# Attention query, key and gate projections of a hybrid encoder block: from 24 full blocks to twelve units of seven half-size products

## The chip, the cores and the metric

The kernel runs on one core of a Trainium2 chip. The metric is the device time of one execution in microseconds (us), taken as the median of several runs. A core has a matrix engine (TensorE, PE in the profile, with its weight loads as PEld), a vector engine (VectorE, DVE), a scalar engine (ScalarE, ACT), GpSimd (POOL) and a sync engine (SyncE, SP). Each takes its own instructions in program order and waits for others by semaphores. SP and POOL issue most of the DMA transfers between device memory (HBM) and the on-chip memory (SBUF); matmul results go to eight banks of PSUM, which PE writes and DVE and ACT read.

## The reference

One layer of an encoder over 512 tokens with 2048 features, in float32. Cut to what matters here:

```python
h = rms_norm(x, norm_mix_w)
q_a, k_a, v_a, q_g, k_g, v_g, r_g, gate_lr = split_cols(h @ w_in, IN_SPLITS)
y_a = chunked_band_attention(q_a, k_a, v_a, att_rel_bias)     # 16 heads of 64
o_g = rms_norm(gated_linear_attention(q_g, k_g, v_g, log_a), gla_norm_w)
y_g = o_g * silu(r_g)                                         # 4 heads, values of 256
x = x + concat([y_a, y_g]) @ w_out
u_gate, u_val = split(causal_depthwise_conv(rms_norm(x, norm_ffn_w) @ w_ffn_up))
x = x + (gelu(u_gate) * u_val) @ w_ffn_down
x = x + sigmoid(rms_norm(x, norm_ple_w) @ w_ple_gate) * (p @ w_ple_proj)
return rms_norm(x, final_norm_w)
```

`q_a`, `k_a`, `v_a` and `r_g` are 1024 features wide each: eight blocks of 128 features for the queries, eight for the keys, eight for the gates `r_g`. With 512 tokens and chunks of 64, the band of nine chunks is causal by chunks: a tile of 128 queries sees the keys up to its own end.

## The kernel before

**How a product is made.** Operands are split into a high part in the fp32r format and a low part, the rest. ACT copies the high part, DVE subtracts to get the low part, and PE adds three products: high by high, high by low, low by high. `wtile` (L108) loads a weight tile of 128x1024 (512 KB) and splits it; `mm3` (L122) issues the three matmuls; `proj` (L127) runs them over the 16 feature blocks of the input, so a projection block of 128 features is 48 matmuls of 128x512 over two weight tiles.

**The front.** The scaled input, split, stays in SBUF as `h1` (16 tiles). The row norm `rb` is multiplied in after the products. In order:

- `vproj` (L218) for the linear attention's values, in two halves of features, tokens on the partitions.
- The linear attention: `gla_proj` (L301) makes query, key and decay of a head; `gla_core` (L349) transposes (`pkt`), forms the inner products (`pat`), the chunk states (`pu`, `S1` to `S3`) and the output (`po`), which is normalised and kept in `onorm`. `gate_block` (L252) 0 and 1 stand ahead of the last head's core.
- `vproj` for the attention's values, into `Va`.
- The attention loop over eight head pairs b, written out by hand so that one pair's softmax runs beside the next pair's projections: `att_q(b)`, `att_transpose` of pair b-1, `att_k(b)`, `att_out` of b-1, `att_probs(b)`. `att_q` and `att_k` (L425, L437) project one block each and split the result by head into `Q`, `Kh`, `Kl` so that score matmuls over 128 rows hold both parts of the queries: `Q` of a head has its high part in its own 64 rows and its low part in the others, `Kh` and `Kl` are in both. `att_probs` (L452) multiplies (`psc`, two matmuls for each of four query tiles, 256, 256, 384 and 512 keys wide), adds the bias `E`, takes the maximum (L467), exponentiates on ACT (L470) and normalises (L472). `att_transpose` (L476) turns the probabilities on PE (`ptr`, ten 128x128 transposes for a head) and ACT copies them to `PT` (L486). `att_out` (L491) multiplies with the values in fp32:

```python
for kt in range(TT):
    for s in range(2):
        c0 = (2 * b + s) * 64
        nc.tensor.matmul(py[s * 64:(s + 1) * 64, kt * P:T], Va[:, kt, c0:c0 + 64], PT[s][:, kt, kt * P:T], ...)
```

- Gate blocks 2 and 3 end the loop. Gate blocks 4 to 7 (`pr` at L62) then alternate with the four blocks of the embedding projection `p @ w_ple_proj` (`pp`, `block_product`, L1090), while `mix_pair` (L1113) forms the operands of the out projection and stores them to HBM.

**The later stages.** The out projection (wo), the up projection, three parts of the down projection and the embedding gate (pg) use a form of Strassen's method with seven products. A `Unit` (L615) makes two blocks of 128 output features: its 256x2048 weight matrix and the 2048x512 input are cut in two by two, and seven products of half size (24 matmuls of 128x256 each) replace the eight. The seven, in order, are P1, P2, P6, P5, P7, P3, P4:

```python
PRODUCTS = {"P1": ("L11", "R11", "A"), "P2": ("L12", "R21", "B"), "P6": ("S2", "N2", "A"), "P5": ("S1", "N1", "C"),
            "P7": ("S3", "T3", "A"), "P3": ("S4", "R22", "C"), "P4": ("L22", "T4", "A")}
```

The first entry is the weight operand: L11, L12, L22 are loaded; S1 = L21 + L22 and S3 = L21 + L11 are loaded with a plain transfer on SP and an accumulating one on POOL's queue; S2 and S4 are sums made on DVE. The second entry is the input operand; `store_pair` (L537) makes its seven forms from two rows of blocks (four differences on DVE) and stores them, and `Stage.load` and `Stage.split` (L592, L598) bring them in and split them. The third is the accumulator bank: P1, P6, P7 and P4 add up in accA, and `collect` (L756) copies or adds the bank's state to a quarter of the result `u` after each of the seven. A product that adds to accA therefore waits for the copy of the one before it.

Products form a list of steps. At each step `prep_high` and `prep_low` split the weights of the step after next, `product` issues the 24 matmuls, `collect` follows, and an `agenda` holds other work to be done at the step: rank 0 (transfers) ahead of the split on ACT, rank 1 between the two halves of the split, higher ranks after the product. On DVE, ACT and PE this program order is kept (`InOrder`, L54; all these instructions carry line L62). Weight pages come from a list `free` of nine (`issue`, L645, loads the next weight when a page comes free); six banks hold accumulators and two are for other work.

Of the kernel before, what the change touches and what calls it, by code (L numbers as in the profile page):

```python
# [14 lines left out]
P = 128  # L15
T = 512
# [13 lines left out]
            "P7": ("S3", "T3", "A"), "P3": ("S4", "R22", "C"), "P4": ("L22", "T4", "A")}  # L30
PLAIN = ("P1", "P2", "P6", "P5", "P7", "P3", "P4")
HALVES = ("P1", "P2", "P6", "P7", "P4", "P5", "P3")
RINGS = {"wr": ("r0", "r1", "r2"), "wh": ("h0", "h1", "h2"), "wl": ("l0", "l1", "l2"), "u": ("u2", "u3", "u0", "u1"),
         "c": ("c1", "c2", "c0"), "x": ("x0", "x1")}
# [5 lines left out]
def encoder_block(ctx: ExitStack, tc: tile.TileContext, A, out):  # L40
# [46 lines left out]

    def page(ring, name, dt=F32, shape=(P, 1024)):
        tags = RINGS[ring]
# [128 lines left out]
    def vproj(src, V, start=False):  # L218
        for c in range(2):
            ps = [psum_mm(f"v{c}_{t}") for t in range(TT)]  # L220
            for kp in range(KD // 2):
                first = start and c == 0
                xs = []
                if first and kp > 0:
                    xs.append(load_input(2 * kp))
                hi, lo = wtile(src[c, kp], f"wv{c}_{kp}", 2 if first and kp < 2 else 1,
                               (lambda: xs.append(load_input(0))) if first and kp == 0 else None)
                if first:
                    xs.append(load_input(2 * kp + 1))
                    sq_acc(xs[0], kp == 0)  # L230
                    sq_acc(xs[1], False)
                    if kp == KD // 2 - 1:
                        first_stats()
                for j in range(2):
                    kt = 2 * kp + j
                    wh = hi[:, j * T:(j + 1) * T]
                    wl = lo[:, j * T:(j + 1) * T]
                    for t in range(TT):
                        sl = slice(t * P, (t + 1) * P)
                        nc.tensor.matmul(ps[t], h1[kt][:, 0, sl], wh, start=kt == 0, stop=False)  # L240
                        nc.tensor.matmul(ps[t], h1[kt][:, 0, sl], wl, start=False, stop=False)  # L241
                        nc.tensor.matmul(ps[t], h1[kt][:, 1, sl], wh, start=False, stop=kt == KD - 1)  # L242
            for t in range(TT):
                nc.scalar.activation(V[:, t, c * T:(c + 1) * T], ps[t], AF.Copy, scale=rtok[:, t:t + 1])
# [5 lines left out]
    onorm = []  # L250

    def gate_block(j):  # L252
        pr = psum_mm("pr")
        proj(pr, [A["w_blk"][24 + j, i] for i in range(2)], h1, f"wr{j}")
        r = tp.tile([P, T], F32, tag="sq", name="r")
        nc.vector.tensor_tensor(r, pr, rb, ALU.mult)
        nc.scalar.activation(r, r, AF.Silu)
        nc.vector.tensor_tensor(onorm[j], onorm[j], r, ALU.mult)

    with ExitStack() as mix:  # L260
        vp = mix.enter_context(tc.tile_pool(name="v", bufs=1, side="right"))

        with ExitStack() as gctx:
            gp = gctx.enter_context(tc.tile_pool(name="gla", bufs=1, side="right"))
            reset = gp.tile([P, T], F32, name="reset")
            nc.gpsimd.memset(reset, 1.0)
            nc.gpsimd.memset(reset.rearrange("p (c j) -> p c j", j=CHUNK)[:, :, 0:1], 0.0)
            causal = gp.tile([P, P], I32, name="causal")
            nc.gpsimd.memset(causal, 1)
            nc.gpsimd.affine_select(causal, causal, pattern=[[1, P]], compare_op=ALU.is_ge, fill=0, base=0, channel_multiplier=-1)  # L270
            attn_t = []
            for i in range(2):
                t = gp.tile([P, T], F32, name=f"attnT{i}")
                nc.gpsimd.memset(t, 0.0)
                attn_t.append(t)

            V = vp.tile([P, TT, 1024], F32, tag="V", name="Vg")
            vproj(A["w_v_g"], V, True)
            up2 = gp.tile([P, T], F32, name="up2")[0:32]
            nc.sync.dma_start(up2, A["gate_up"])  # L280

            gl = page("wr", "wgate_r")
            nc.sync.dma_start(gl[:, :256], A["w_gate"])
            glh = page("wh", "glh", F32R)
            nc.scalar.activation(glh[:, KD * 32:KD * 32 + 96], attn_t[0][:, 0:96], AF.Copy)
            gl3 = gl[:, :256].rearrange("p (k r) -> p k r", r=16)
            g3 = glh[:, :KD * 32].rearrange("p (k r) -> p k r", r=32)
            nc.scalar.activation(g3[:, :, 0:16], gl3, AF.Copy)
            nc.vector.tensor_tensor(g3[:, :, 16:32], gl3, g3[:, :, 0:16].bitcast(F32), ALU.subtract)
            plr = psum_mm("plr")  # L290
            for kt in range(KD):
                w = glh[:, kt * 32:kt * 32 + P]
                nc.tensor.matmul(plr, w, h1[kt][:, 0, :], start=kt == 0, stop=False)
                nc.tensor.matmul(plr, w, h1[kt][:, 1, :], start=False, stop=kt == KD - 1)
            lr = gp.tile([P, T], F32, name="lr")[0:32]
            nc.vector.tensor_tensor(lr, plr[0:32, :], rb[0:32, :], ALU.mult)

            def gt(name, tag, bufs=1, cols=T):
                return gp.tile([P, cols], F32, tag=tag, name=name, bufs=bufs)

            def gla_proj(hd):  # L301
                pz = psum_aux("pz")
                nc.tensor.matmul(pz, up2[:, hd * P:(hd + 1) * P], lr, start=True, stop=True)
                b = bgate[:, hd:hd + 1]
                e = gt("e", "e")
                nc.scalar.activation(e, pz, AF.Abs, bias=b)
                nc.scalar.activation(e, e, AF.Exp, scale=-1.0)
                nc.scalar.activation(e, e, AF.Ln, bias=1.0)
                m = gt("lf", "lf")
                nc.vector.tensor_scalar(m, pz, b, 0.0, ALU.add, ALU.min)  # L310
                nc.vector.tensor_tensor(m, m, e, ALU.subtract)
                cs = gt("cs", "cs")
                nc.vector.tensor_tensor_scan(cs, reset, m, 0.0, ALU.mult, ALU.add)
                cs3 = cs.rearrange("p (c j) -> p c j", j=CHUNK)
                last = cs3[:, :, CHUNK - 1:CHUNK]
                eb = gt("eb", "eb", 2)
                nc.scalar.activation(eb, cs, AF.Exp, scale=1.0 / TAU)
                en = gt("en", "en", 2)
                nc.scalar.activation(en, cs, AF.Exp, scale=-1.0 / TAU)
                dd = gt("dd", "dd", 2)  # L320
                nc.vector.tensor_tensor(dd.rearrange("p (c j) -> p c j", j=CHUNK), cs3,
                                        last.broadcast_to([P, NCH, CHUNK]), ALU.subtract)
                nc.scalar.activation(dd, dd, AF.Exp, scale=-1.0 / TAU)
                dec = gt("dec", "dec", 2, NCH)
                nc.scalar.activation(dec, last, AF.Exp, scale=1.0 / TAU)
                dec2 = gt("dec2", "dec2", 2, 2 * NCH + TT)
                de = dec.rearrange("p (t c) -> p t c", c=2)
                to_end = dec2[:, 0:NCH].rearrange("p (t c) -> p t c", c=2)
                from_start = dec2[:, NCH:2 * NCH].rearrange("p (t c) -> p t c", c=2)
                nc.vector.memset(dec2[:, 0:2 * NCH], 1.0)  # L330
                nc.vector.tensor_copy(to_end[:, :, 0:1], de[:, :, 1:2])
                nc.vector.tensor_copy(from_start[:, :, 1:2], de[:, :, 0:1])
                nc.vector.tensor_tensor(dec2[:, 2 * NCH:].rearrange("p (t c) -> p t c", c=1), de[:, :, 0:1], de[:, :, 1:2],
                                        ALU.mult)

                pk = psum_mm("pk")
                proj(pk, [A["w_blk"][20 + hd, i] for i in range(2)], h1, f"wkg{hd}")
                kf = gt("kf", "kf")
                nc.vector.tensor_tensor(kf, pk, rb, ALU.mult)
                nc.vector.tensor_tensor(en, kf, en, ALU.mult)  # L340
                nc.vector.tensor_tensor(dd, kf, dd, ALU.mult)
                pq = psum_mm("pq")
                proj(pq, [A["w_blk"][16 + hd, i] for i in range(2)], h1, f"wqg{hd}")
# [1004 lines left out]
```

## Time and profile before

| | |
|---|---|
| median of 3 runs | 2341.88 us (2335.12 to 2343.68) |
| the profiled execution, its own time | 2345.5 us |
| its span, first to last instruction | 2343.8 us |
| mean granted clock of PE | 0.993 |
| 0 to 338.05 us (values, linear attention) | 338.05 us, PE busy 336.85 |
| 338.05 to 600.47 us (attention loop with gate blocks 2, 3) | 262.42 us, PE busy 261.54 |
| 600.47 to 668.12 us (gate blocks 4 to 7, embedding projection) | 67.65 us, PE busy 66.55 |
| 668.12 to 2343.80 us (out, up, down projections, embedding gate) | 1675.68 us, PE busy 1637.16 |

Times of a trace are from the first instruction of the profiled execution. "PE busy" counts the time in which at least one matmul record is open; records of pipelined matmuls overlap, so the mean length of one is more than its share of the time. A row of the chain gives the start, the length, the engine, the tile written, the line, and how many instructions the piece holds; fp32 matmuls leave two records each. In the list of groups "out<-in" names what is written and read.

### The profile page before, as it was taken

What the parts mean: (1) busy time and instruction counts of PE and PEld (TensorE: products, weight loads), DVE (VectorE), ACT (ScalarE), POOL (GpSimd) and SP (SyncE); (2) the same over time, 40 slices, a digit from 0 to 9 for tenths busy, and PEclk for the clock granted to TensorE, in tenths of its full rate; (3) what the DMA queues carried; (4) which work ended last, traced back from release to release, by engine and by line L of the source; (5) the groups of instructions that cost most, each with busy time, mean ns of one, the idle gap of its engine ahead of it and who ended that gap; (6) DMA issues with size and microseconds to landing.
All of it is one profiled execution on the core that took longest, in us unless ns stands there. A gap on an engine that the chain in (4) does not pass through costs nothing.

```text
span 2343.8 us, 42271 instructions
## 1 busy us (share of the span) xinstructions
PE 2302.1 (98%) x16924; PEld 2162.6 (92%) x16924; DVE 1787.1 (76%) x2459; ACT 1231.7 (53%) x1807; POOL 122.7 (5%) x156
## 2 busy tenths in 40 slices
PE   9999999999999999999999999999999999999996
PEld 8878887777789999999999999999989999999995
DVE  6356326665578898898888888888888787898987
ACT  6344235544465565555555555555564554656655
POOL 0000000000000010000000100000000100001100
PEclk9999999999999999999999999999999999999998
DMA  5222323322788987777777777777875977879994
GB/s 203 83 72 72 101 98 102 92 89 84 235 294 253 299 244 203 211 218 214 214 205 217 207 217 209 209 213 200 252 242 189 311 235 230 280 248 329 280 276 163
DMA packets 172821, 473.99 MB, mean 202 GB/s; under 512 B 18736, under 2 KB 58928, under 8 KB 172624
## 3 DMA queue, kind: packets, MB, share of 16 engines
q1 hardware_dynamic: 148112, 392.64, 48.0%
q0 software_dynamic: 20160, 72.36, 17.9%
q10 hardware_dynamic: 4352, 6.29, 0.8%
q8 instruction: 132, 2.16, 0.4%
q14 instruction: 65, 0.53, 0.1%
HBM read 404.11 MB, written 65.01 MB: 200 GB/s over the span
## 4 chain that ended last, share of the span: by engine, by line
PE 90%; DVE 4%; ACT 3%; DMA 2%; issue 1%; DVEq 0%; SPq 0%; ACTq 0%; POOL 0%; POOLq 0%
PE accA L62 36%; PE accC L62 18%; PE accB L62 9%; PE v L240 2%; PE v L242 2%; PE v L241 2%; PE pr L62 2%; PE pqa L124 1%; PE pqa L123 1%; PE pka L125 1%; PE pqa L125 1%; PE pka L123 1%; PE pka L124 1%; PE pp L62 1%; DMA s<-in_w_dn 1%
## 5 line engine op out<-in xcount | busy, mean ns | idle before, releaser
L62 DVE TENSOR_TENSOR wl<-s,wh 128x1024 fp32r<-128x1024 f32 (+1 forms) x317 | 379.4, 1197 | 62.8 <-ACT wh L62 62.4
L62 DVE TENSOR_TENSOR wl<-l,wh 128x1024 fp32r<-128x1024 f32 (+1 forms) x268 | 319.5, 1192 | 52.1 <-ACT wh L62 51.9
L62 ACT ACTIVATE wh<-l 128x1024 fp32r<-128x1024 f32 (+1 forms) x268 | 276.9, 1035 | 143.5 <-PE accC L62 100.6
L62 ACT ACTIVATE wh<-s 128x1024 fp32r<-128x1024 f32 (+1 forms) x317 | 327.9, 1035 | 28.7 <-DVE s L62 12.0
L62 ACT ACTIVATE u<-accA 128x256 f32<-128x256 f32 x254 | 96.4, 380 | 362.4 <-PE accA L62 362.2
L62 DVE TENSOR_TENSOR s<-s,l 128x1024 f32<-128x1024 f32 (+1 forms) x168 | 200.4, 1193 | 1.4 <-DMA s<-in_w_dn 1.4
L62 PE MATMUL accA<-up_T,wh 128*128 128x256 f32 x1408 | 180.2, 280 | 0.0
L62 PEld LDWEIGHTS accA<-up_T,wh 128*128 128x128 f32 x1408 | 171.9, 188 | 0.0
L62 DVE SCALAR_TENSOR_TENSOR cv<-u,cw,cv 128x511 f32<-128x511 f32 (+1 forms) x176 | 131.6, 748 | 3.1
L663 POOL DMA_DIRECT2D s<-in_w_up x88 | 75.1, 853 | 795.5 <-DMA s<-in_w_up 337.9
L119 DVE TENSOR_TENSOR wv_l<-wv_r,wv_h 128x1024 fp32r<-128x1024 f32 (+1 forms) x34 | 39.5, 1161 | 84.2 <-ACT wv_h L118 84.1
L240 PE MATMUL v<-wv_h,h 128*128 128x512 f32 x256 | 100.5, 393 | 0.0
L242 PE MATMUL v<-wv_h,h 128*128 128x512 f32 x256 | 100.1, 392 | 0.0
L241 PE MATMUL v<-wv_l,h 128*128 128x512 f32 x256 | 99.8, 390 | 0.0
L62 PE MATMUL accA<-up_T,wl 128*128 128x256 f32 x704 | 97.1, 280 | 0.0
L62 PE MATMUL accB<-up_R,wh 128*128 128x256 f32 x704 | 91.7, 282 | 2.0 <-DVE up_R L62 1.3
L62 PE MATMUL accA<-dn_T,wh 128*128 128x256 f32 x704 | 90.7, 281 | 2.7 <-ACT wh L62 2.7
L62 PE MATMUL accA<-up_R,wh 128*128 128x256 f32 x704 | 90.4, 281 | 0.0
L62 PE MATMUL accC<-up_R,wh 128*128 128x256 f32 x704 | 90.0, 280 | 0.0
L62 PE MATMUL accA<-up_N,wh 128*128 128x256 f32 x704 | 90.0, 280 | 0.0
L62 PE MATMUL accC<-up_N,wh 128*128 128x256 f32 x704 | 90.0, 280 | 0.0
L62 PEld LDWEIGHTS accB<-up_R,wh 128*128 128x128 f32 x704 | 87.1, 190 | 2.6 <-DVE up_R L62 1.5
(394 smaller groups left out, 5287.7 us busy)
## 6 DMA issues: line engine op xcount, KB each, us to landing
l<-in_w_up SPq DMA_DIRECT2D x132, 512.0 KB, 5.3
s<-in_w_up SPq DMA_DIRECT2D x88, 512.0 KB, 4.7
s<-in_w_up POOLq DMA_DIRECT2D x88, 512.0 KB, 6.1
l<-in_w_dn SPq DMA_DIRECT2D x56, 448.0 KB, 4.9
l<-in_w_out SPq DMA_DIRECT2D x28, 512.0 KB, 5.4
l<-in_w_dn SPq DMA_DIRECT2D x28, 512.0 KB, 4.9
l<-in_w_ple_gate SPq DMA_DIRECT2D x24, 512.0 KB, 7.0
g_R<-cv SPq DMA_DIRECT2D x66, 128.0 KB, 4.8
```

The lines of the kernel that those rows point to most:

```text
L62: ins = f(*args, **kw)
L119: nc.vector.tensor_tensor(lo[:, c], raw[:, c], hi[:, c].bitcast(F32), ALU.subtract)
L123: nc.tensor.matmul(po, whi, act[:, 0, :], start=start, stop=False)
L124: nc.tensor.matmul(po, whi, act[:, 1, :], start=False, stop=False)
L125: nc.tensor.matmul(po, wlo, act[:, 0, :], start=False, stop=stop)
L240: nc.tensor.matmul(ps[t], h1[kt][:, 0, sl], wh, start=kt == 0, stop=False)
L241: nc.tensor.matmul(ps[t], h1[kt][:, 0, sl], wl, start=False, stop=False)
L242: nc.tensor.matmul(ps[t], h1[kt][:, 1, sl], wh, start=False, stop=kt == KD - 1)
L663: nc.gpsimd.dma_start(t, src("L22" if name == "S1" else "L11"), accum_op=ALU.add)
```

## The change

The 16 query and key blocks and the eight gate blocks become a stage of twelve units in the seven-product form: units 0 to 7 are the query and key blocks of a head pair, units 8 to 11 two gate blocks each. The rest follows from that:

- The products need the normed input in the seven forms. `input_pair` multiplies the input by `nmix` and `rb` during the second half of the linear attention's value projection (eight times two multiplies and four differences on DVE) and stores 56 pieces of 128 KB to `h1d`. The forms R11, R21, N2 are loaded and split during the attention's value projection; the other eight tiles of 512 KB (N1, T3, R22, T4) are loaded when `h1` is no longer needed, and split at the first step.
- The attention's values go to HBM (`vad`, eight stores of 256 KB) and come back as 256 KB for a head pair. The first half of that projection now stands where gate blocks 0 and 1 stood.
- The linear attention's outputs go to HBM (`ond`) and are reloaded by `after_gates`, which applies silu and multiplies.
- Attention becomes agenda items, counted in steps from the end of the unit. `high` and `low` split by head; the second copy of `Kh` and `Kl` for the other 64 rows is made by four SBUF to SBUF transfers on POOL's queue (`double`) instead of on ACT and DVE. Scores, softmax, transposes and values are spread over steps 5 to 12. Head 0's value matmuls are in step 9, head 1's in step 11.
- The embedding projection is four steps behind unit 11, and the out projection's operands are loaded and split beside units 11 and these.
- Until the last attention item the front has six weight pages, three accumulator banks, one bank for the attention output (b3) and four for scores, transposes and the rest; then `attention_done` gives back three pages and three banks. The rows of `w_out` are permuted on the host to match the new pairing of blocks.

The later stages stay as they are. The diff, cut to its core:

```diff
-    def gate_block(j):
-        pr = psum_mm("pr")
-        proj(pr, [A["w_blk"][24 + j, i] for i in range(2)], h1, f"wr{j}")
...
+    aux_tags = ["b4", "b5", "b6", "b7"]
...
+            if single:
+                self.groups = [[u] for u in self.units]
+                return
...
+    free = [f"r{i}" for i in (3, 4, 5)]
...
+    banks = [f"b{i}" for i in range(3)]
...
+    def attend(unit):
+        b, M = unit.u, {}
+        o = unit.o
...
+        def high():
...
+            for s in range(2):
+                a = slice(s * 64, s * 64 + 64)
+                act.activation(M["Q", s][a], o[a, 0, :], AF.Copy, scale=0.125)
+                act.activation(M["Kh", s][a], o[a, 1, :], AF.Copy)
+
+        def low():
+            for s in range(2):
+                a, z = slice(s * 64, s * 64 + 64), slice(64 - s * 64, 128 - s * 64)
+                vec.scalar_tensor_tensor(M["Q", s][z], o[a, 0, :], 0.125, M["Q", s][a].bitcast(F32), ALU.mult, ALU.subtract)
+                vec.tensor_tensor(M["Kl", s][a], o[a, 1, :], M["Kh", s][a].bitcast(F32), ALU.subtract)
+
+        def double():
+            for s in range(2):
+                a, z = slice(s * 64, s * 64 + 64), slice(64 - s * 64, 128 - s * 64)
+                for n in ("Kh", "Kl"):
+                    nc.gpsimd.dma_start(M[n, s][z], M[n, s][a])
...
+        def values(s):
+            if s == 0:
+                M["y"] = pp_.tile([P, T], F32, tag="b3", name="py")
+            pt = M["PT", s]
+            for kt in range(TT):
+                x = pt[:, kt, kt * P:T] if kt < 3 else pt[:, 1, 0:P]
+                ten.matmul(M["y"][s * 64:(s + 1) * 64, kt * P:T], M["V"][:, kt, s * 64:(s + 1) * 64], x, start=kt == 0,
+                           stop=kt == TT - 1)
...
+        items = [(1, 0, lambda: load_e(0)), (2, 2, high), (3, 0, lambda: load_e(1)), (3, 1, low), (3, 3, double),
+                 (4, 1, lambda: mask(0)), (5, 0, load_v), (5, 1, lambda: mask(1)), (12, 1, result)]
+        if b % 2:
+            items.append((13, 1, lambda: store_pair(mixd, b // 2, ypair[0][:, 0, :], ypair[0][:, 1, :])))
+        for s in range(2):
+            for h in range(2):
+                t = 5 + 2 * s + h
+                items += [(t, 6, lambda s=s, h=h: scores(s, h)), (t + 1, 1, lambda s=s, h=h: soft(s, h)),
+                          (t + 2, 1, lambda s=s, h=h: normal(s, h)), (t + 2, 5, lambda s=s, h=h: turn(s, h)),
+                          (t + 3, 1, lambda s=s, h=h: evict(s, h))]
+            items.append((9 + 2 * s, 4, lambda s=s: values(s)))
+        return items
...
+    def front_weights(u, q):
+        j = {"1": u, "2": 8 + u}[q[1]] if u < 8 else 24 + 2 * (u - 8) + (q[1] == "2")
+        return A["w_blk"][j, int(q[2]) - 1]
+
+    front = Stage("in", list(range(12)), 8, h1d, front_weights, lambda u: (attend if u.u < 8 else after_gates)(u), "dma",
+                  "dma", single=True)
...
+    for n, p in enumerate(PLAIN):
+        op = PRODUCTS[p][1]
+        if n > 2:
+            for g in range(2):
+                agenda[(n - 3) // 2 if g else 0].append((3, lambda op=op, g=g: front.split(op, g)))
...
+            def input_pair(k):
+                for i in (k, k + 8):
+                    x = xslot(i, "")
+                    vec.scalar_tensor_tensor(x, x, nmix[:, i:i + 1], rb, ALU.mult, ALU.mult)
+                store_pair(h1d, k, xslot(k, ""), xslot(k + 8, ""), gp.tile([P, 1024], F32, tag="tp", name="tp", bufs=2))
...
-            gate_block(0)
-            gate_block(1)
+            values_a(0)
             gla_core(3, *st)
...
+    values_a(1, operand_step)
+    hctx.close()
...
+    for op in ("N1", "T3", "R22", "T4"):
+        for g in range(2):
+            front.load(op, g)
+    free += ["r0", "r1", "r2"]
+    issue()
+    prep(0)
+    prep(1)
```

More of the change, by code (lines that the diff above doesn't have):

```diff
@@ L1056, in norm_root @@
         norm["w"] = rstd_begin(norm["ms"])
-    for e in (vec, act, ten):
-        e.on = True
-    wo = stages[0]
-    nc.sync.dma_start(cw, A["conv"])
-    pt = page("x", "pT").rearrange("p (k t) -> p k t", k=2)
-    nc.sync.dma_start(pt, A["p"].rearrange("k p t -> p k t"))
-    ps_ = xtile("N2", 1, "ps").rearrange("p h (k t) -> p k h t", k=2)
-    blocks = []
-    for j in range(4, 8):
-        blocks += [("gate", j, 0), ("gate", j, 1), ("ple", j - 4, 0)]
-    raws, ready, sums = {}, {}, {}
@@ L1161, in encoder_block @@
+    nc.gpsimd.memset(pad, 0.0)
+    for op in ("N1", "T3", "R22", "T4"):
+        for g in range(2):
+            front.load(op, g)
+    free += ["r0", "r1", "r2"]
+    issue()
+    prep(0)
+    prep(1)
     pctx.close()
@@ L1163, in encoder_block @@
     aux[0] = aux_bank
-    free += ["r0", "r1", "r2"]
-    issue()
+    actx = ExitStack()
+    att.append(actx.enter_context(tc.tile_pool(name="att", bufs=1, side="right", reuse_waits="tile")))
+    use_rings(FRONT_RINGS)
+    epage = pg.tile([P, 2, T], F32, tag="r7", name="bias")
+    eopen["page"] = [epage[:, s, :] for s in range(2)]
+    for e in (vec, act, ten):
+        e.on = True
     for i, (unit, prod) in enumerate(steps[:-4]):
```

725 lines of the change are left out of this document (346 added, 379 removed).

## The prediction

> **What bounds the kernel now.** I began with the page: busy time of each engine, then the chain that ended last.
>
> ```profile
> span 2343.8 us, 42271 instructions
> PE 2302.1 (98%) x16924; PEld 2162.6 (92%) x16924; DVE 1787.1 (76%) x2459; ACT 1231.7 (53%) x1807; POOL 122.7 (5%) x156
> PE 90%; DVE 4%; ACT 3%; DMA 2%; issue 1%; DVEq 0%; SPq 0%; ACTq 0%; POOL 0%; POOLq 0%
> ```
>
> PE is busy 98% of the span and carries 90% of the chain. A change pays if it takes matmul time away without opening holes in PE. Next I read the chain in order of time over the stages that the change touches (columns: start, length, what ran; x24 counts the matmuls of the piece).
>
> ```profile
> 49.29 0.86 PE pb L62 x2
> ...
> 407.63 0.85 PE ptr L485 x7
> ...
> 418.04 2.30 PE py L496 x16
> ...
> 436.55 0.39 ACT PT L486
> 436.99 0.44 PE ptr L485 x2
> ...
> 584.50 1.78 PE ptr L485 x16
> ...
> 600.47 0.47 issue
> 600.93 1.23 DVE wb_l L62
> 602.20 10.73 PE pr L62 x46
> ...
> 618.53 10.92 PE pr L62 x48
> ...
> 668.12 9.30 DMA wo_N<-mix_N
> ...
> 694.84 5.60 PE accA L62 x48
> ```
>
> A projection block of 48 matmuls of 512 columns takes 10.92 us. A half-size product of 24 matmuls of 256 columns in the out projection takes 5.60/2 = 2.80. All eight value matmuls of a head pair (16 records) take 2.30. The same chain in the up projection:
>
> ```profile
> 1001.65 2.83 PE accC L62 x24
> ```
>
> Last, busy time by stretch (length, then PE, PEld, DVE, ACT, POOL, clock, DMA share, GB/s): two head pairs, the end of the front, the start of the out projection, a steady piece of the up projection.
>
> ```profile
> 404.05:434.10 30.05, 29.96 (x150) 23.26 (x148) 18.23 (x55) 15.36 (x34) 0.00 (x0) 1.00 0.31 93
> 434.10:464.15 30.05, 29.96 (x149) 23.25 (x148) 18.22 (x55) 15.36 (x34) 0.00 (x0) 1.00 0.32 92
> 602.20:668.12 65.92, 65.89 (x286) 53.64 (x286) 39.18 (x62) 27.65 (x40) 3.67 (x5) 1.00 0.98 325
> 668.12:724.80 56.68, 53.77 (x451) 52.96 (x452) 49.45 (x65) 36.95 (x59) 0.85 (x1) 1.00 0.79 248
> 920.00:1320.00 400.00, 400.00 (x3399) 400.00 (x3398) 352.40 (x421) 212.74 (x288) 34.16 (x40) 1.00 0.78 212
> ```
>
> A head pair takes 30.05 us. Its two blocks are 21.84, so its attention part is 8.21. The up projection runs with no hole in PE while DVE is busy 352.4/400 = 88% and DMA moves 212 GB/s: that is the load this product form can carry.
>
> **The change, term by term, against the profiled execution of 2345.5 us.**
>
> *Products (A).* 24 blocks go: 24 x 10.92 = 262.1 us. 12 units of 7 products come: 84 products at 2.80 to 2.83 are 235.2 to 237.7. A = -24.4 to -26.9; I take -25.7.
>
> *Value matmuls (B).* Before, the loop alternates the two heads, which write to rows 0 to 63 and 64 to 127 of one bank. One head streams 512+384+256+128 = 1280 fp32 columns. A full-width fp32 matmul of 512 columns takes 0.86 (the pb row), so one head alone should cost 2.15 and both in turn 4.30. The measured 2.30 for both says that the heads ran side by side. The change puts head 0 nine steps and head 1 eleven steps after the unit, with whole-array products between: no partner is left. B = 8 x (4.30 - 2.30) = +16.0; bounds 0 (if a neighbouring matmul overlapped after all) to +16, what switching adds being counted under D. The Trainium skill, page "TensorEngine Tiling (Array Packing)", sections "Overview" and "Tiling Modes", says that with a stationary free dimension of 64 or less the array can be used as independent tiles, for up to twice the speed, and that a change of tiling mode drains it. That speaks against this part of the change; the trace's 2.30 against 4.30 (1.9 times) agrees, and by the page's full factor of two B would be 8 x 2.15 = +17.2.
>
> *Entry into the first unit (C).* In the instruction order after, P1 and P2 follow the last attention-value matmul at once: their operands were loaded beside it. P6 adds to the accumulator that P1 wrote, so it waits until ACT has copied P1 out. That copy stands on ACT behind six operand splits, whose loads follow four 256 KB stores of attention values on SP and wait for the space that the last value matmuls free. The sixth split needs the seventh of eight 512 KB loads.
>
> ```profile
> l<-in_w_up SPq DMA_DIRECT2D x132, 512.0 KB, 5.3
> 669.80 1.04 ACT L62 ACTIVATE wh<-l 128x1024 fp32r<-128x1024 f32 x1
> 671.93 0.39 ACT L62 ACTIVATE u<-accA 128x256 f32<-128x256 f32 x1 [1.09 <-PE accA L62]
> ```
>
> The top rate in the windows is 325 GB/s at share 0.98: 1.6 us for each load, so seven loads are 11.3 and the stores 3.2 more. With the order's waits the seventh load lands 12.5 to 17 us after the last value matmul; one split (1.04) and the copy (0.39) follow; two products (5.6) cover. PE idles 8.3 to 12.8 us; I take 11. Queued behind the copy are only later copies and splits of the same units. After the one idle stretch of this kind at the end of the kernel the granted clock drops:
>
> ```profile
> 2310.00:2315.00 5.00, 2.92 (x19) 2.71 (x18) 4.26 (x10) 2.82 (x7) 0.00 (x0) 0.86 0.00 0
> 2315.00:2320.00 5.00, 5.00 (x30) 4.53 (x30) 2.79 (x4) 4.82 (x9) 0.00 (x0) 0.80 0.00 0
> ```
>
> 5 x (0.14 + 0.20) = 1.7 us lost. C = 11 + 1.7 = +12.7; bounds 8.3 to 14.5.
>
> *Waits within attention (D).* Of the 8.21 us, values are 2.30. Transposes are 20 x 1.78/16 = 2.23. Score matmuls stream 256+256+384+512 = 1408 columns four times (two heads, high and low part), at 10.92/(48 x 512) us for a column 2.50. That leaves 1.18 us per pair, 9.4 over eight, in which PE waits, for instance for the copy of PT at 436.55. The new steps put one to four other products between the links of that chain, so these waits can go: bound -9.4. New: ten groups per unit switch between product and attention matmuls, with waits for banks. The same 1.18 spread over more places, up to twice that, is my upper bound, +9.4. I take 0.
>
> *Waits around it (E).* The hole before the gate blocks (0.47 + 1.23 at 600.47) goes: -1.7. The out projection's start loses 56.68 - 53.77 = 2.91 now, behind operand loads that land in 9.30. After, the same operand loads stand behind the gate units and the embedding products at the same DMA load: unchanged, bounds -2.9 to +5.
>
> *Linear attention's last head (F).* Before, two attention-value matmuls lie between its state updates and its output; after, none, and on VectorE an operand split stands between the first and the second state.
>
> ```profile
> 246.63 0.58 PE L240 MATMUL v<-wv_h,h 128*128 128x512 f32 x1
> 247.05 0.40 PE L241 MATMUL v<-wv_l,h 128*128 128x512 f32 x1
> ...
> 246.69 1.06 DVE L383 SCALAR_TENSOR_TENSOR S<-S,dec,pu 128x256 f32<-128x256 f32 x2
> ```
>
> A split is 1.23 (as at 600.93), twice the chain's own 0.53, and 0.5 of cover is gone: 0 to +3; I take +1.5.
>
> *Edits at nothing.* The normed input is formed, differenced and stored during the second half of the linear attention's value projection:
>
> ```profile
> 50.00:95.00 45.00, 45.00 (x200) 37.27 (x199) 9.00 (x8) 11.94 (x16) 0.00 (x0) 1.00 0.26 85
> ```
>
> DVE has 36 us free there. Eight pairs cost two multiplies and four differences each, at most 6 x 0.7 = 4.2 us, 34 us if none overlap: full, not over; uncovered it costs up to 3. Within a unit DVE goes from 18.2 us to about 24: three more splits (3.7), two sums (2.4), four additions of 0.42 (1.7), half a store pair (0.8), less two scaled evictions, two low halves and the y copy (3.4), and margin. In a unit of about 29 us that is 83%, under the 88% that the up projection bears. The unit's weights (seven 512 KB transfers) with bias, values and four copies are 4.9 MB, 170 GB/s, under 212.
>
> Sum: -25.7 + 16.0 + 12.7 + 0 - 1.7 + 1.5 = +2.8, a profiled execution of 2348.3. The execution profiled now lies 3.6 above the median of its runs (2341.88), so the forecast for the median is 2344.7. Differences under 0.5% (11.7 us) I count as no change, which is about what a measurement of this kernel can tell apart.
>
> **Rivals.**
>
> *Attention hides better than I allow (faster).* D's 9.4 us vanish, C is at its lower end without clock loss (-4.4), F is nothing (-1.5): 2348.3 - 15.3 = 2333.0, median 2329.4. For it: the steps lie one to four products of 2.8 us apart, against links like the PT copy of 0.39. Against: no stage now mixes products with fp32 matmuls, so no row shows this without holes. If B were wrong as well, it would be 16 lower.
>
> *The third weight sum arrives late (slower).* S1 of every unit is a plain load, then an accumulating load on the POOL queue, and the front has six weight pages where the later stages have nine.
>
> ```profile
> s<-in_w_up SPq DMA_DIRECT2D x88, 512.0 KB, 4.7
> s<-in_w_up POOLq DMA_DIRECT2D x88, 512.0 KB, 6.1
> ...
> s<-in_w_out SPq DMA_DIRECT2D x4, 512.0 KB, 9.9
> s<-in_w_out POOLq DMA_DIRECT2D x4, 512.0 KB, 12.0
> ```
>
> The chain is 10.8 us at up's loads and 21.9 at those of the out projection's start. In the order after, the page for the next S1 comes free about five products ahead of the one that uses the sum; with the attention matmuls between them that is some 16 us, less 1.23 for its split: an estimate, by which the rival decides from about 15 us on. On POOL the four copies of K halves stand among these transfers, and scores wait for them. Half-way between the two loads, 16.4, each of the twelve units loses about 1.5; at 18.5, 3.5. The second gives 12 x 3.5 = 42 less the half of it that also covers D's and E's waits: about +25, 2373, median 2370. Against: 170 GB/s is a lighter load than up's.
>
> *It does not do what it says.* The products may be saved but given back elsewhere whole: if the out projection's start loses 5 more and the input pairs 3, the result is 2356, median 2353, still within my band's edge.
>
> **How the numbers follow.** No change, from C and B eating A: 0.45, own range 2332 to 2354, the last rival in it. Faster: 0.25. Slower: 0.30, since more of the unpriced items are waits than gains. The range takes the faster rival with E's gain (2329.4 - 2.9 - some of B, 2323) and the slower one with a little margin: 2323 to 2371.
>
> **What would show it.** Products of 2.80 to 2.83 in the front and 12 units of 7 (A). Value matmuls of about 2.15 us for each head (B; 1.15 refutes it). One hole of 8 to 13 us in PE at the third product of the first unit, ended by ACT's copy of accA (C). Attention units of 28 to 29.5 us (D), the first and the last longer. Holes ended by a DMA of s1 on POOL, or at every unit's fourth product, would show the slower rival. The forecast is wrong if PE's idle time in the front is under 5 us or over 30.

## The result

The changed kernel takes 2350.83 us (median of 9 runs, 2347.77 to 2360.10) against 2342.43 for the kernel before, run beside it. The ratio is 1.0037 with a 95% interval of 1.0023 to 1.0051: a small loss, inside the band of 0.5% that the prediction called no change, and inside its range. The forecast was 2344.7. A second set of runs of the same kernel gave 1.0049 (1.0030 to 1.0067). Both intervals reach past 0.5%: what the runs show is a small loss near the edge of that band.

The first execution profiled after the change took 2360.1, the longest of its nine. The same matmuls run in one of two cadences 1% apart, and which one a stage gets differs from trace to trace (last section). In the up projection that moves a time by some 8 us; so the parts below are compared by their places in the traces, ahead of that stage, and the medians stand beside them.

The page of the changed kernel, busy time and chain:

```profile
span 2358.3 us, 44593 instructions
PE 2296.9 (97%) x17788; PEld 2200.7 (93%) x17788; DVE 1882.2 (80%) x2564; ACT 1289.5 (55%) x1909; POOL 161.1 (7%) x212
...
PE 64%; DVE 3%; ACT 2%; DMA 1%; issue 1%; SPq 0%; ACTq 0%; DVEq 0%
```

PE is busy 5.2 us less than before, the span is 14.5 longer, and so PE is idle 19.7 us more. Most of the products' gain has gone into other busy time of PE, the separated heads above all, and the holes take more than the rest. What PE waited for between 230 and 720 us (total, times, longest):

```profile
PE accA L64 <- ACT u L64: 9.3, 1, 9.3
PE pp L64 <- ACT pp_o L64: 6.5, 3, 3.4
PE accA L64 <- ACT wo_R L64: 2.5, 1, 2.5
PE ptr L64 <- DVE sc L64: 1.7, 1, 1.7
PE pp L64 <- DVE ps L64: 1.1, 1, 1.1
PE accA L64 <- ACT pair_c L253: 0.8, 1, 0.8
```

They are at three places: the entry into the first unit (9.3 and 0.8), the first transposes of the first attention unit (1.7), and the embedding products with the first out product behind them (6.5, 1.1 and 2.5). No wait names a weight sum or a POOL transfer. The same by stretch, in the changed kernel: the twelve units, the embedding products, the out projection, the up projection.

```profile
317.09:648.00 330.91, 318.87 (x2432) 293.77 (x2433) 252.90 (x555) 203.24 (x403) 36.65 (x54) 0.98 0.76 215
648.00:680.54 32.54, 25.00 (x98) 18.88 (x97) 17.27 (x22) 19.47 (x31) 3.41 (x4) 0.95 0.97 300
680.54:840.60 160.06, 157.33 (x1345) 156.92 (x1344) 131.74 (x167) 91.95 (x136) 8.71 (x11) 1.00 0.82 259
840.60:1681.80 841.20, 839.16 (x7107) 838.15 (x7106) 727.96 (x877) 452.29 (x622) 73.21 (x86) 1.00 0.76 211
```

and the last two of them in the kernel before:

```profile
668.78:829.10 160.32, 158.07 (x1345) 157.26 (x1346) 137.72 (x176) 96.43 (x144) 8.52 (x10) 1.00 0.88 275
829.10:1670.30 841.20, 839.16 (x7107) 838.10 (x7106) 727.59 (x877) 452.95 (x622) 72.86 (x86) 1.00 0.77 211
```

Out and up projection are the same to 0.3 us in these two executions. The out projection starts at 680.54 instead of 668.78, 11.8 later: that is what the change costs. The other 2.7 us of the two spans arise behind the up projection, in stages that the change leaves alone.

### The profile page after: what moved, and what is told of

It reads as the page before. It is cut to its first block, busy times and chain, and to the rows that moved or that the text cites. A ratio compares the mean times of both kernels' runs of the same rounds, so it can differ in the third digit from the quotient of the medians.

```text
span 2358.3 us, 44593 instructions
## 1 busy us (share of the span) xinstructions
PE 2296.9 (97%) x17788; PEld 2200.7 (93%) x17788; DVE 1882.2 (80%) x2564; ACT 1289.5 (55%) x1909; POOL 161.1 (7%) x212
## 4 chain that ended last, share of the span: by engine, by line
PE 64%; DVE 3%; ACT 2%; DMA 1%; issue 1%; SPq 0%; ACTq 0%; DVEq 0%
PE accA L64 36%; PE accC L64 19%; PE accB L64 9%; DVE wl L64 1%; DMA l<-in_w_ple_gate 1%; DVE u L64 0%; PE pp L64 0%; DVE s L64 0%; DVE xs L64 0%; DMA s<-in_w_dn 0%; ACT wh L64 0%; DVE root L64 0%; DVE x L64 0%; ACT u L64 0%; DMA pg_T<-h_T 0%
## 5 line engine op out<-in xcount | busy, mean ns | idle before, releaser
L64 DVE TENSOR_TENSOR wl<-s,wh 128x1024 fp32r<-128x1024 f32 (+1 forms) x365 | 438.1, 1201 | 76.3 <-ACT wh L64 75.1
L64 DVE TENSOR_TENSOR wl<-l,wh 128x1024 fp32r<-128x1024 f32 (+1 forms) x308 | 368.0, 1195 | 70.8 <-ACT wh L64 70.4
L64 ACT ACTIVATE wh<-l 128x1024 fp32r<-128x1024 f32 (+1 forms) x308 | 319.1, 1037 | 174.6 <-PE accC L64 118.6
L64 ACT ACTIVATE wh<-s 128x1024 fp32r<-128x1024 f32 (+1 forms) x365 | 378.0, 1036 | 34.4 <-DVE s L64 13.3
L64 ACT ACTIVATE u<-accA 128x256 f32<-128x256 f32 x290 | 109.7, 378 | 382.6 <-PE accA L64 382.0
L64 DVE TENSOR_TENSOR s<-s,l 128x1024 f32<-128x1024 f32 (+1 forms) x192 | 229.9, 1197 | 6.9 <-DMA s<-in_w_blk 6.9
L64 DVE TENSOR_TENSOR u<-u,accC 128x256 f32<-128x256 f32 x98 | 41.0, 419 | 85.3 <-PE accC L64 84.0
L64 PEld LDWEIGHTS accA<-dn_T,wh 128*128 128x128 f32 x704 | 86.8, 190 | 3.8 <-ACT wh L64 3.8
```

What stands on the lines that cost most here:

```text
L64: ins = f(*args, **kw)
```

## The experiments

Each was run beside the kernel before. The table gives, from each trace, where the embedding products, the out and the up projection begin, and then the median and the ratio to the kernel before.

| kernel | embedding | out | up | median | ratio (95%) |
|---|---|---|---|---|---|
| before | (mixed in) | 668.8 | 829.1 | 2342 to 2344 | 1 |
| changed | 648.0 | 680.5 | 840.6 | 2350.83 | 1.0037 (1.0023 to 1.0051) |
| again | 648.5 | 681.2 | 842.6 | 2353.23 | 1.0049 (1.0030 to 1.0067) |
| heads_joined | 631.8 | 665.5 | 825.6 | 2337.43 | 0.9982 (0.9968 to 0.9996) |
| joined_in_turn | 642.1 | 675.0 | 836.6 | 2351.54 | 1.0043 (1.0027 to 1.0059) |
| splits_spread | 638.6 | 672.2 | 832.3 | 2345.74 | 1.0022 (1.0007 to 1.0036) |
| four_banks | 646.3 | 672.9 | 836.7 | 2351.50 | 1.0045 (1.0029 to 1.0061) |
| embedding_mended | 644.6 | 668.0 | 826.5 | 2343.01 | 0.9999 (0.9985 to 1.0013) |
| joined_spread | 629.0 | 661.6 | 824.3 | 2336.18 | 0.9979 (0.9962 to 0.9997) |
| all_three | 627.2 | 650.6 | 809.1 | 2326.11 | 0.9934 (0.9918 to 0.9950) |
| all_stores_last | 626.2 | 649.7 | 808.1 | 2324.82 | 0.9926 (0.9908 to 0.9944) |

### again: the changed kernel a second time

> The changed kernel once more, with a second profile. In its first profile the entry into the first unit has a hole of 9.3 us in PE, the embedding products wait 10 us in all, and everything from the up projection on is 3 us longer than before; that execution (2360.1) lay 9 us above the median (2350.8). If the embedding waits are a matter of transfers that land by chance early or late, a second profile shows them with another length and the hole at the entry with nearly the same (8 to 11 us). If they are set by the order of the instructions, both come back within 1 us. Ratio to the kernel before 1.002 to 1.005.

The hole at the entry was 9.5 us, the waits on `pp_o` 6.7, the wait on `wo_R` 2.5, against 9.3, 6.5 and 2.5. So they are not transfers that land early or late by chance. What in the order of the instructions sets them is shown by the edits below.

### heads_joined and joined_in_turn: the two heads' value matmuls

In both, head 1's probabilities go to three tiles of their own (`acc` and two temporaries, free at that time), which takes ACT one copy for each 128 columns, six more for a unit.

```diff
-        def values(s):
-            if s == 0:
-                M["y"] = pp_.tile([P, T], F32, tag="b3", name="py")
-            pt = M["PT", s]
+        def values():
+            M["y"] = pp_.tile([P, T], F32, tag="b3", name="py")
             for kt in range(TT):
...
+                for s in range(2):
+                    pt = M["PT", s]
...
-            items.append((9 + 2 * s, 4, lambda s=s: values(s)))
+        items.append((11, 4, values))
```

`joined_in_turn` swaps the two loops: head 0's four matmuls, then head 1's.

> Both heads' value matmuls in one step (step 11), alternating as in the kernel before; head 1's probabilities go to three tiles of their own. My theory: a lone head costs 2.15 us, the two side by side 2.3, so eight units get 2.0 us back each, 16 us: ratio to before about 0.997 (2351 - 16 = 2335), value matmuls of a unit 2.3 to 2.4 in one stretch. Rival: the heads' price is hidden or made elsewhere (the interleaving of PE's work with products overlaps a lone head as well, or ACT's six more copies for each unit, about 1 us, take it back): ratio within 0.002 of that of the changed kernel.

> As heads_joined (both heads' value matmuls in step 11, head 1's probabilities in three tiles), but head 0's four matmuls and then head 1's four, where heads_joined alternates. If the two heads run side by side only when their matmuls alternate, the stretch takes 4.3 to 4.6 us for a unit (2.7 to 3.2 in heads_joined) and the ratio goes back to that of the changed kernel, 1.004 or a little above for ACT's extra copies. If what heads_joined won came from one group of value matmuls instead of two (fewer changes between kinds of matmul, a shorter hold of the bank), the order within the step does not matter and the ratio stays at 0.998.

In the changed kernel a lone head's eight records, and what follows on PE (timeline: start, length of the piece):

```profile
443.89 2.37 PE L64 MATMUL py<-PT,va 128*64 128x512 f32 x8
446.19 0.76 PE L64 MATMUL ptr<-ident,sc 128*128 128x128 f32 x5
```

The next matmul begins 2.30 us after the first: one head alone takes as long as both took in the kernel before (2.30 for x16). In the chain of heads_joined, both heads:

```profile
444.99 3.08 PE py L64 x13
448.07 3.00 PE accC L64 x24
```

and in the chain of joined_in_turn:

```profile
448.36 2.30 PE py L64 x8
450.66 0.10 issue
450.76 1.46 PE py L64 x6
452.22 3.04 PE accC L64 x24
```

Both heads take 4.60 apart, 3.86 (452.22 - 448.36) in turn, in every unit and less than the 4.3 to 4.6 expected, and 3.08 alternating here. Alternating, the units differ. One unit earlier in heads_joined (timeline; `acc` holds head 1's probabilities):

```profile
417.06 0.64 PE L64 MATMUL py<-PT,va 128*64 128x512 f32 x1
417.42 0.64 PE L64 MATMUL py<-acc,va 128*64 128x512 f32 x1
...
419.72 1.45 PE L64 MATMUL accC<-in_R,wh 128*128 128x256 f32 x10
```

The stretch takes 2.66 (419.72 - 417.06) here and in every other unit, 3.08 to 3.11 in the ones between, and 2.30, as in the kernel before, in the last. Head 1's first matmul starts 0.36 us after head 0's here, about 0.8 after it in the long ones, and together with it in the last; what delays it was not tried. Over eight units this is 36.8 us apart, 30.9 in turn and 22.6 alternating.

The order within the step matters, as the theory said. Head 0 in turn takes 2.30, and head 1 then only 1.56: its first matmuls ran beside head 0's last. Against the changed kernel the out projection starts 15.0 us earlier when they alternate and 5.5 earlier in turn; the medians show 13.4 for the first (15.8 against the second set) and none for the second. So the separation of the heads is worth 13 to 16 us, and alternation more than half of it; what the mere joining gives is seen in the trace only. Head pairs' periods in heads_joined are

```profile
403.47:430.81 27.34, 27.34 (x223) 25.99 (x221) 22.78 (x59) 17.58 (x45) 3.94 (x6) 1.00 0.80 204
430.81:459.05 28.24, 27.98 (x223) 25.91 (x221) 24.02 (x63) 20.07 (x51) 3.94 (x6) 1.00 0.75 191
```

27.8 on the mean, against 29.36 in the changed kernel, 1.6 less instead of 2.0. Every other unit has 20.07 us of work on ACT and 0.26 of open holes in PE.

### splits_spread: the entry into the first unit

```diff
-                agenda[(n - 3) // 2 if g else 0].append((3, lambda op=op, g=g: front.split(op, g)))
+                agenda[n - 2].append((3, lambda op=op, g=g: front.split(op, g)))
```

> The eight late operand splits stand one pair for each step (steps 1 to 4) instead of six at step 0, so that the copy of accA after the first product is not behind them on ACT. My theory: the hole of 9.3 us at the third product and the 2.4 us of slower clock behind it go; new holes of at most 2 us where a product still waits for its own operand's load. 9 to 12 us less than the changed kernel: ratio to before 0.999. Rival: the hole is set by the loads themselves, not by the place of the copy, and returns at the fourth product at the same length: ratio unchanged at 1.0037.

The changed kernel's entry, in the timeline (in brackets: idle time of the engine before it, and what ended it):

```profile
331.66 1.06 ACT L64 ACTIVATE in_T<-in_T 128x1024 fp32r<-128x1024 f32 x1 [1.50 <-DMA in_T<-h_T]
332.62 0.36 ACT L64 ACTIVATE u<-accA 128x256 f32<-128x256 f32 x1
333.04 3.78 PE L64 MATMUL accA<-in_N,wh 128*128 128x256 f32 x16 [9.30 <-ACT u L64]
```

The sixth split waits for its transfer, the copy of accA waits behind it, and PE waits for the copy. The 16 matmuls behind the hole take 3.78 us; 2.14 is what 16 take at the start of the first product. In splits_spread the longest wait left in the first unit is at its seventh product:

```profile
336.00 2.35 DVE L64 TENSOR_TENSOR in_T<-in_T 128x1024 fp32r<-128x1024 f32 x2
338.27 0.41 DVE L64 TENSOR_TENSOR u<-u,accA 128x256 f32<-128x256 f32 x1
338.83 2.12 PE L64 MATMUL accA<-in_T,wh 128*128 128x256 f32 x16 [2.15 <-DVE u L64]
```

The embedding starts 9.4 earlier and the out projection 8.3 earlier; the medians differ by 5 to 7.5 us. The place of the copy set the hole: the rival is out. The estimate of 9 to 12 was high, since new holes of over 3 us remain (2.2, 0.7 and 0.3). The longest is the same fault on another engine: the sum `u<-u,accA`, which frees accA, stands on DVE behind two operand splits, and DVE is busy 14.05 of the 14.12 us from 324.15 to 338.27. `all_stores_last` moves the four value stores behind the eight loads on SP:

> As all_three, and the four stores of attention values stand behind the eight operand loads on SP instead of ahead of them. With the splits spread, 4 us of holes are left in the first unit, each where an operand landed late. If the stores' 1 MB and their 1.2 us of issue are what delays the loads, 2 to 3 us of these go. Rival: the loads alone are the limit (4 MB at 325 GB/s are 12.9 us against 11.2 us of products ahead of the last two), then under 1 us.

Up starts 1.0 us earlier than in all_three and the hole of 2.2 stays:

```profile
337.25 3.65 PE L64 MATMUL accA<-in_T,wh 128*128 128x256 f32 x16 [2.17 <-DVE u L64]
```

Neither the theory nor the rival holds. In this trace no operand split on ACT waits for a load any more (in all_three three do), and yet the hole is as long: by the trace it is the order on DVE that sets it, as in splits_spread, and not a load that lands late. An edit to that order was not tried.

### four_banks and embedding_mended: the embedding products

> The embedding products use four PSUM banks in turn instead of two. If PE waits there because ACT copies the banks out late, behind operand splits of the out projection, and two banks give 2.8 us of lead only, four banks give 5.6 and most of the 6.5 us of waits on these copies go: 4 to 7 us less than the changed kernel. Rival: ACT itself is late for the whole stage (splits, copies, and output pages whose stores land after 11 us), the lead is used up once and the out projection starts as late: under 2 us.

```diff
-            pp = psum_aux("pp")
+            tag = ("b6", "b7", banks[-1], banks[-2])[i]
+            pp = pp_.tile([P, T], F32, tag=tag, name="pp")
```

The waits on `pp_o` fell from 6.5 to 2.1, and the wait on `wo_R` behind them rose from 2.5 to 5.0. The out projection began 7.6 earlier and the up projection only 3.9; the median did not move. By the median the rival was right for this edit; by the traces 3.9 us are left at the up projection, between the two. The timeline of four_banks shows why:

```profile
675.03 1.09 ACT L64 ACTIVATE pp_o<-pp 128x512 f32<-128x512 f32 x2 [1.59 <-DMA ppd<-pp_o]
676.57 1.58 ACT L64 ACTIVATE wo_T<-wo_T 128x1024 fp32r<-128x1024 f32 x2 [0.46 <-ACT pp_o L64]
678.36 0.71 ACT L64 ACTIVATE wo_R<-u 128x256 fp32r<-128x256 f32 x2
678.82 2.29 PE L64 MATMUL accA<-wo_R,wh 128*128 128x256 f32 x9 [4.96 <-ACT wo_R L64]
```

ACT waits for an output page whose store has not landed, and then splits wo_T, which only a later product needs, ahead of wo_R, which PE waits for. The next edit mends both:

```diff
-                o = page("c", "pp_o").rearrange("p (s t) -> p s t", s=2)
+                n = 2 * unit.u + i // 2
+                o = (pg.tile([P, 1024], F32, tag=f"u{n - 3}", name="pp_o") if n in (3, 4) else page("c", "pp_o"))
...
-                agenda[i0 + max(10 + n // 2, 12 if late_one else 0)].append((4, lambda op=op: wo.split(op, 1, False, (1,))))
+                agenda[i0 + (9 if n < 2 else ...)].append((2 if n < 2 else 4, lambda op=op: wo.split(op, 1, False, (1,))))
...
-    agenda[i0 + 6].append((1, embedding_split))
+    agenda[i0 + 5].append((1, embedding_split))
```

> Four things at the embedding stage alone: four banks for its products, five pages instead of three for its output, the out projection's first two operand tails split one step earlier and ahead of the loads that ACT waits for, the split of its own input one step earlier. With four banks alone PE waited 5.0 us for ACT at the first out-projection product, because ACT waited 1.6 us for a page whose store had not landed and then split a late operand first. My theory: ACT's order and pages are what is late, so with these mended the embedding's 16 products take close to their 22.4 us again (32.5 in the changed kernel) and the out projection keeps most of the lead: 6 to 9 us less than the changed kernel. Rival: the operands' transfers set the time (DMA share 0.92 to 1.0 here), the out projection then waits for them and the gain stays under 3 us.

The stage fell from 32.54 to

```profile
644.60:668.00 23.40, 22.78 (x98) 17.81 (x97) 16.34 (x24) 17.93 (x30) 3.40 (x4) 1.00 1.05 345
```

at a DMA share of 1.05 (0.97 in the changed kernel): the transfers run at least as full as before and hold nothing up. The up projection begins 14.1 earlier, and the median is 7.8 lower (10.2 against the second set). Of the 14.1, 3.4 arise already ahead of the embedding, in units that are the same code; there the first transposes waited 0.6 us instead of 1.7, and the clock stayed at 1.00 behind them (last section). Here the theory was right and the rival out. Beyond the banks alone, the four edits were not tried apart.

### joined_spread and all_three: the parts together

> The heads joined and the entry's splits spread, both at once. If the two losses are independent, the parts add: by the traces 15.0 (joined) and 8.3 (spread) less until the out projection starts, so 23 us less than the changed kernel there, and about 2328 in the median (ratio 0.994). If one gain was only lent (the front waits then for weights, six pages, or ACT, which has the extra copies), the sum is short by 4 us or more and the trace shows new waits in the units.

> Joined, spread, and the embedding mended. If the embedding stage is late by its own order, this takes 6 to 9 us more from the sum of the two: 2320 to 2323, ratio 0.991. If transfers set the start of the out projection, then with a faster front they come no earlier and the gain is at most 3: 2326.

joined_spread starts the out projection 18.9 us earlier than the changed kernel, 4.4 short of the sum of 23.3, and its median (2336.18) is 1.3 lower than that of heads_joined alone, where 9 were expected. In this profile the out projection runs in the slower cadence, 162.7 us against 160.1 in the changed kernel. New in its waits is

```profile
PE psc L64 <- DMA Kl<-Kl: 2.4, 2, 1.4
```

the second copies of the keys on POOL's queue, at 390 and at 503 us. all_three, with the same front, has no such wait, and `again` has one of 0.4 with the hole still there, so it varies between executions. The cause of the rest of the 4.4 is open. With the embedding mended as well, the out projection starts 29.9 earlier, and the time is 0.9934 of the kernel before (0.9918 to 0.9950). That is 10.1 less than joined_spread, so the embedding's gain is there; the median of 2326.11 meets the rival's 2326 by accident, since that was reckoned from about 2328 for joined_spread, which took 2336. all_three, and all_stores_last with 0.9926 (0.9908 to 0.9944), beat both kernels; between these two the runs show no difference.

## Why the prediction was right, and where it was off

The forecast of no change came true, mainly for the reason given: the products' gain is eaten by the separated heads and by the hole at the entry. The sum was +2.8; the trace has +11.8 up to the out projection and the medians +8.4. That this stayed within the band (11.7 us) is partly luck, because a loss of 10.1 us at the embedding products was not in the sum. By its terms:

| term | predicted | measured |
|---|---|---|
| A, products | -25.7 (-24.4 to -26.9) | a gate unit of seven is 19.60 (heads_joined) to 19.79 (changed) against 21.84: -24.6 to -26.9 |
| B, value matmuls | +16.0 | a lone head 2.30, so 8 x (4.60 - 2.30) = +18.4 by the stretch; 13 to 16 come back when joined |
| C, entry | +12.7 (hole 11, clock 1.7) | hole 9.3, clock 2.7 (below), 0.8 at the very first product: +12.8 |
| D, waits within attention | 0 (-9.4 to +9.4) | about -2.6 |
| E, waits around it | -1.7 | -1.7 + 10.1 = +8.4 |
| F, last linear head | +1.5 | +0.9 (last value matmul ends at 317.09; before, 338.05 - 21.84 = 316.21) |

*A* held; 19.60 and 19.79 are seven products of 2.80 and of 2.83, the two cadences of the last section. *B* had the mechanism right and the size wrong: a lone head takes 2.30 where the pb row, 0.86 for 512 columns, gave 2.15, and the 18.4 lie outside its bounds of 0 to +16. *C* was right in mechanism and size; the hole was shorter and the clock's part longer.

*D.* A steady attention unit takes

```profile
407.70:437.06 29.36, 29.36 (x222) 26.35 (x221) 22.71 (x59) 17.47 (x40) 3.93 (x6) 1.00 0.72 190
437.06:466.43 29.37, 29.37 (x223) 26.36 (x222) 23.99 (x63) 19.90 (x46) 3.95 (x6) 1.00 0.69 184
```

with seven products (19.60), values (4.60), scores (2.50) and transposes (2.23): 0.43 is left, against 1.18 before, so -0.75 for each of eight. The first attention unit lost about 3.4 of these 6.0 again, 1.7 in a wait for the first transposes and as much in a slower clock after it. The faster rival was right in that these waits mostly go. DVE is busy 77% to 82% of a unit (22.71/29.36, 23.99/29.37; the prediction had 83%), and PE has no hole there.

*E is the step that failed*: "the same operand loads stand behind the gate units and the embedding products at the same DMA load: unchanged, bounds -2.9 to +5". The loads were not what set it. The change also takes the embedding's products from four banks to two and its output from four pages to three, and places the out projection's splits on ACT between their copies. That costs 32.54 - 4 x 5.60 = 10.1 us (before, a block of 24 matmuls of 512 columns takes 5.60), twice the upper bound; 7.5 of it is idle time of PE. four_banks and embedding_mended show that the banks, the pages and ACT's order set it together, and not the transfers.

The slower rival, a late S1, did not occur: no wait of PE in the front names a weight sum. The last rival came nearest in place and size: it named the out projection's start, and the loss arose just ahead of it, in the embedding products. It gave no cause for it, and the 3 us for the input pairs did not come (F). PE's idle time in the front is 12.0 + 7.5 = 19.6 us by the stretches, between the 5 and 30 that the prediction named.

## What to carry to other kernels

Before a loop is taken apart into steps, look for pairs of instructions in it that run side by side on halves of one engine: here the price of pulling them apart was over half of what the new form of the products saved. A copy that frees an accumulator belongs on its engine ahead of any split that waits for a transfer; the 2.2 us left in the first unit, a sum on DVE behind two splits, are of the same kind. When a stage moves, carry its banks and pages with it into the sum, and not its matmuls and loads alone: two banks and one page fewer, with other work placed between the copies, cost nearly as much as the hole that the prediction had looked for.

## What the runs showed of the hardware

**Holes of 1.7 and 2.2 us in PE that brought the clock to half, and others that did not.** Windows of the changed kernel around the first transposes (length, busy times, then the granted clock as third from the end):

```profile
373.00:374.00 1.00, 0.40 (x4) 0.20 (x2) 0.96 (x4) 1.00 (x4) 0.00 (x0) 1.00 0.47 164
374.00:375.00 1.00, 0.00 (x0) 0.00 (x0) 0.96 (x4) 1.00 (x4) 0.00 (x0) 1.00 0.82 328
375.00:376.00 1.00, 0.82 (x6) 0.59 (x6) 0.93 (x6) 0.35 (x1) 0.00 (x0) 0.95 0.11 41
376.00:377.00 1.00, 1.00 (x3) 0.81 (x4) 0.97 (x5) 0.87 (x3) 0.00 (x0) 0.50 0.00 0
...
378.00:379.00 1.00, 1.00 (x7) 1.00 (x6) 0.96 (x4) 1.00 (x4) 0.00 (x0) 0.50 0.54 201
379.00:380.00 1.00, 1.00 (x9) 1.00 (x9) 0.93 (x7) 0.68 (x3) 0.00 (x0) 0.84 0.00 0
```

PE is idle for 1.7 us and at work again from 375.10. The clock falls about 0.8 us later and stays at half for some 3.4 us. Around the hole of 9.3 us it is at half in the latter part of the hole and for 5 us behind it:

```profile
329.00:332.00 3.00, 0.00 (x0) 0.00 (x0) 2.36 (x2) 1.40 (x2) 0.00 (x0) 0.50 0.99 392
332.00:335.00 3.00, 1.96 (x9) 1.97 (x10) 2.26 (x2) 3.00 (x5) 0.00 (x0) 0.50 0.10 38
335.00:338.00 3.00, 3.00 (x16) 3.00 (x16) 3.00 (x5) 1.76 (x2) 0.00 (x0) 0.50 0.49 168
338.00:341.00 3.00, 3.00 (x26) 3.00 (x26) 2.95 (x3) 1.45 (x2) 0.00 (x0) 0.94 0.32 109
```

(338.00 - 333.04) x 0.50 + 3 x 0.06 = 2.7 us lost. The Trainium skill, page "TensorE: Matmul & The Clock Gate", Part 1, has the clock at half after at least one idle window of about 3.4 us. The 0.50 and the 3.4 us agree; holes of 1.7 us here and of 2.2 at the same place in `again` were enough, so the rule of a whole idle window does not cover them.

The length of the hole alone does not decide either. At the same transposes the clock stayed at 1.00 behind holes of 1.4 us (four_banks) and 1.6 (all_stores_last). And four traces have a hole of 2.2 us at the seventh product of the first unit: in all_three and all_stores_last the clock fell to 0.50 behind it, in splits_spread and joined_spread it stayed at 1.00. The lines shown above for that product have the price: the 16 matmuls behind the hole take 3.65 us in all_stores_last and 2.12 in splits_spread. What decides was not tried.

**The same matmuls in two cadences.** In the up projection, with PE busy throughout and the granted clock at 1.00, the kernel before (profiled execution) and all_three:

```profile
1000.00:1300.00 300.00, 300.00 (x2549) 300.00 (x2549) 263.16 (x314) 158.87 (x215) 25.61 (x30) 1.00 0.78 213
```

```profile
1000.00:1300.00 300.00, 300.00 (x2574) 300.00 (x2573) 263.56 (x317) 161.20 (x218) 25.59 (x30) 1.00 0.77 216
```

2549 against 2574 matmuls: 1% slower, with the same matmuls in the same order, through nearly the whole stage (841.2 us in the kernel before, 833.8 in all_three). A weight split takes the same time in both stretches, 1220 ns on DVE and 1053 on ACT, so it is PE's pace that differs. In the up projection the faster cadence came in the profiles of four of the changed versions, the slower in the other six and the kernel before. It goes by stage and not by execution: the prediction's two prices of a product, 2.80 and 2.83, come from the out and the up projection of one execution, and joined_spread has the slower cadence in the out projection and the faster in the up projection. The 26 runs of the kernel before in the first set of experiments spread from 2334.9 to 2348.8, which this would explain; what sets the cadence was not tried.
